# Recurrence levels 2 to 16 as products of 32 stationary and 16 moving columns

## Chip, core and metric

The kernel runs on one core of a Trainium2 chip. The metric is the device time of one execution in microseconds (us); lower is better. Three runs of the kernel before are given by their median, lowest and highest time. A profile is one further execution under the hardware profiler, with a time of its own.

## What is computed

The program is one block of a hybrid encoder: 512 tokens, model width 2048. A root-mean-square norm, one input projection of 5120 columns, a pooling mixer on the first 1024 of them, a gated linear recurrence (HGRN2) with 8 heads of 128 on the rest, an output projection, a residual, and a dense layer of 8192 with squared ReLU and a second residual. The change lies in the recurrence alone, whose part inside a chunk is a decayed score matrix:

```python
b = jnp.cumsum(g_c, axis=2)
o_inter = jnp.einsum('bhtd,bhde->bhte', q_c * jnp.exp(b), state)
diff = b[:, :, :, None, :] - b[:, :, None, :, :]
decay = jnp.exp(jnp.where(causal, diff, -jnp.inf))
scores = jnp.einsum('bhtd,bhsd,bhtsd->bhts', q_c, k_c, decay)
o_intra = jnp.einsum('bhts,bhse->bhte', scores, v_c)
```

The decay between a query t and a key s differs in each of the 128 channels d, so that the scores are not one plain product of q and k.

## The kernel before

**Order of the whole.** TensorE's work is, in order: ten groups of input projections (`pj`, line 251), four groups of output projections (`om`, line 251 too), and the dense layer's products (`mi`, `ps`, `al`, `ga`; lines 1059 to 1280). All of it is laid out by hand in program order; each engine runs its own instructions in that order and waits on semaphores.

**What runs between the projections.** A `Clock` holds generators ("tasks"). After each block of a projection group, which is twelve products of 128 x 128 stationary and 512 moving columns, `clock.tick()` advances every task by one step. The recurrence of four heads (a chunk `c` of the class `Hgrn`, two of them) is such a task: its `scores` generator begins once `evac_q` has its first block, and issues one step per tick. So each of its steps stands between two blocks of `pj` products on TensorE, and its VectorE and ScalarE work stands among the splitting of the projection weights into a high and a low part (`wh` on ScalarE, line 210; `wl` on VectorE, line 211).

**The score matrix by levels.** The 512 tokens are four windows of 128 (`NT` = 4). `ST` holds, per head and window, the 128 x 128 scores with keys on partitions and queries along the free axis. `LEVELS` is 1, 2, 4, 8, 16, 32, 64. At level m a window is cut into blocks of 2m tokens, and the second m tokens of a block (queries) meet the first m (keys). `decay` then multiplies queries and keys by the gates of a half block, so that after level m both carry the decay up to their block's border and level 2m can use them as they are. The diagonal and level 1 are made by column products and sums (`col_products`, `col_sums`), not by `level`.

**One burst of `level(m, hp)`** does a pair of heads, `hp`. For m up to 16 it issues 8 products (2 heads x 4 windows): all 128 keys of the window are stationary, and the 64 tokens that are queries at this level are the moving columns. Most of the 128 x 64 result is of no use; `merge` copies the wanted entries into `ST` on VectorE by `copy_predicated` with `masks[m]` (line 645). For m = 32 it issues 16 products of 32 stationary and 32 moving columns, written to the partitions 0 to 31 and 64 to 95 of the result; for m = 64, 8 products of 64 and 64. There ScalarE copies the wanted rows into `ST` (line 642). The result tile `lps` comes from the four rotating PSUM buffers of the pool `pss`. All these products are in plain float32, and the profile shows two weight loads and two matmul records for each of them.

**Around it.** A burst needs the queries and keys that the same pair's `decay` of the level before left, two ticks earlier; `decay` (lines 627, 629, 631 on VectorE) waits for the burst that read them. `ST` is read by `outputs` (products `po`, lines 679 and 681). GpSimd builds the masks and some edge values in the first microseconds, and has nothing else to do until the pooling mixer's second chunk and the first loads for the output stage.

Of the kernel before, what the change touches and what calls it, by code (L numbers as in the profile page):

```python
# [8 lines left out]
F32 = mybir.dt.float32  # L9
F32R = mybir.dt.float32r  # L10
U32 = mybir.dt.uint32
AF = mybir.ActivationFunctionType
ALU = mybir.AluOpType
# [3 lines left out]
P = 128  # L17
T = 512
NT = T // P
# [9 lines left out]
def hybrid_block(  # L29
# [20 lines left out]
    nc = tc.nc  # L50
# [17 lines left out]
    hgp = hg.__enter__()  # L68
    late = {}

    def junk_tile(shape, name):
        if "tp2" in late:
            return late["tp2"].tile(shape, F32, tag="junk", bufs=1, name=name)
        return hgp.tile(shape, F32, tag="junk", bufs=2, name=name)
# [11 lines left out]
    masks = {}  # L86
    for m in LEVELS[:-2]:
        nb = 64 // m
        mk = hgp.tile([P, nb, m], F32, name=f"mask{m}")
        nc.gpsimd.memset(mk, 1.0)  # L90
        nc.gpsimd.affine_select(out=mk, in_=mk, compare_op=ALU.is_ge, fill=0.0,
                                base=0, pattern=[[-2 * m, nb], [0, m]], channel_multiplier=1)
        nc.gpsimd.affine_select(out=mk, in_=mk, compare_op=ALU.is_ge, fill=0.0,
                                base=m - 1, pattern=[[2 * m, nb], [0, m]], channel_multiplier=-1)
        masks[m] = mk
    edge = {}
    for w in (2, 4, 8, 16):
        e = hgp.tile([P, w], F32, name=f"edge{w}")
# [425 lines left out]
    class Hgrn:  # L524
# [39 lines left out]
        def scores(self):  # L564
            F, Q, K = self.F, self.Q, self.K
            self.ST = hgp.tile([P, 4, NT, P], F32, tag="ST", name=f"ST{self.c}")

            sc = hgp.tile([P, 2, 2, 512], F32R, tag="V", name=f"sc{self.c}")

            def col_products(i, a, b):  # L570
                pr = junk_tile([P, 512], "pr")
                nc.vector.tensor_tensor(out=pr.rearrange("p (h x) -> p h x", h=a.shape[1]), in0=a, in1=b, op=ALU.mult)
                nc.scalar.copy(out=sc[:, i, 0], in_=pr)
                nc.vector.tensor_tensor(out=sc[:, i, 1], in0=pr, in1=sc[:, i, 0].bitcast(F32), op=ALU.subtract)

            def col_sums(i):
                ps = pss.tile([P, 512], F32, tag="s", name="cps")
                nc.tensor.matmul(ps, ones_r, sc[:, i, 0], start=True, stop=False)
                nc.tensor.matmul(ps, ones_r, sc[:, i, 1], start=False, stop=True)
                return ps  # L580

            def diag(h):
                nc.vector.tensor_tensor(out=self.ST[:, h], in0=col_sums(h % 2).rearrange("p (w t) -> p w t", t=P),
                                        in1=ident.unsqueeze(1).to_broadcast([P, NT, P]), op=ALU.mult)

            def halves(x, hp, k):
                return x[:, 2 * hp:2 * hp + 2].rearrange("p h (b two) -> p h b two", two=2)[:, :, :, k]

            for h in range(4):
                col_products(h % 2, Q[:, h:h + 1], K[:, h:h + 1])  # L590
                nc.vector.tensor_tensor(out=Q[:, h], in0=Q[:, h], in1=F[:, h], op=ALU.mult)
                yield 2
                diag(h)
            for hp in range(2):
                col_products(hp, halves(Q, hp, 1), halves(K, hp, 0))
                self.decay(1, hp)
                yield 2
                self.merge(1, hp, col_sums(hp))
            for m in LEVELS[1:]:
                for hp in range(2):  # L600
                    self.level(m, hp)
                    yield 1

        def level(self, m, hp):
            nb = 64 // m
            hs = slice(2 * hp, 2 * hp + 2)
            Q, K = self.Q[:, hs], self.K[:, hs]
            ps = pss.tile([P, 2, NT, nb, m], F32, tag="s", name="lps")
            mb = m if m >= 32 else P
            for h in range(2):  # L610
                for w in range(NT):
                    for r in range(0, P, 2 * m if m >= 32 else P):

                        b0, b1 = (r // (2 * m), r // (2 * m) + 1) if m >= 32 else (0, nb)
                        rhs = Q[:, h, w * P:(w + 1) * P].rearrange("p (b two i) -> p b two i", two=2, i=m)
                        nc.tensor.matmul(ps[r:r + mb, h, w, b0:b1], K[:, h, w * P + r:w * P + r + mb],  # L616
                                         rhs[:, b0:b1, 1, :], start=True, stop=True)
            self.decay(m, hp)
            self.merge(m, hp, ps.rearrange("p h w b i -> p (h w b i)"))

        def decay(self, m, hp):

# [748 lines left out]
    for k in range(n_in, len(slots)):  # L1371
        g, i, q = slots[k]
# [58 lines left out]
```

## Time and profile before

| what | value |
|---|---|
| median of three runs | 1961.36 us (1960.89 to 1961.70) |
| profiled execution, its own time | 1961.64 us |
| span of its instructions | 1959.9 us |
| TensorE matmul busy | 1941.4 us, 10040 records |
| VectorE busy | 1281.7 us |
| ScalarE busy | 841.9 us |
| GpSimd busy | 146.2 us |
| bursts of `lps` on TensorE | 172.2 to 429.3 us, 448 matmul records |

A matmul record is one pass of TensorE over the moving columns; its duration covers the whole way through the array, so that records of a dense stream overlap, and the distance from start to start is what one of them costs. Weight loads are listed as an engine of their own (PEld), since they run beside matmuls. A row of the timeline merges equal instructions that follow each other: its second column is the time from the first one's start to the last one's end.

### The profile page before, as it was taken

The page shows a single profiled execution, that of the slowest core. Times are in us where ns is not written, and L with a number is a line of the kernel's source. Part 1 is how long each engine was busy: PE and PEld are TensorE (multiplying, and loading weights), DVE is VectorE, ACT ScalarE, POOL GpSimd, SP SyncE. Part 2 cuts the span into 40 slices and gives each one's busy share as a digit, 9 for nine tenths or more (in the row PEclk, how much of TensorE's full clock was granted, in tenths as well). Part 3 has the DMA queues.
Part 4 walks back from the last instruction along what each step waited for, and adds up shares of the span by engine and source line. Part 5 has one row for each costly group of instructions (what it writes and reads, how often), then busy time and mean ns, then how long its engine had stood idle before and what let it go on. Part 6 is the DMA issues. An engine that isn't in the chain of part 4 may idle for free.

```text
span 1959.9 us, 24431 instructions
## 1 busy us (share of the span) xinstructions
PE 1941.4 (99%) x10040; PEld 1656.5 (85%) x10040; DVE 1281.7 (65%) x1414; ACT 841.9 (43%) x1009; POOL 146.2 (7%) x228
## 2 busy tenths in 40 slices
PE   9999999999999999999999999999999999999996
PEld 7888888888888899988888888888888888888885
DVE  5647543753632388566665766677777878878877
ACT  6221232223232277444444444445544444444454
POOL 1000000000000001101111011011010010010010
PEclk9999999999999999999999999999999999999999
DMA  8231213211252468988889789898897897898896
GB/s 312 86 106 67 83 68 108 86 65 65 100 212 86 148 200 180 248 233 203 216 219 213 226 215 207 240 235 238 211 245 225 199 235 230 206 229 223 217 228 134
DMA packets 56208, 355.00 MB, mean 181 GB/s; under 512 B 6048, under 2 KB 7072, under 8 KB 18336
## 3 DMA queue, kind: packets, MB, share of 16 engines
q0 software_dynamic: 25056, 162.54, 39.7%
q1 hardware_dynamic: 30752, 190.37, 26.5%
q8 instruction: 79, 1.29, 0.3%
q10 hardware_dynamic: 288, 0.52, 0.1%
q14 instruction: 33, 0.27, 0.0%
HBM read 328.24 MB, written 25.17 MB: 180 GB/s over the span
## 4 chain that ended last, share of the span: by engine, by line
PE 96%; DVE 1%; ACT 1%; issue 0%; DMA 0%; SPq 0%; DVEq 0%; ACTq 0%
PE pj L251 22%; PE ps L1059 18%; PE al L1280 17%; PE ga L1280 13%; PE ps L1062 9%; PE om L251 9%; PE mi L1074 4%; PE lps L616 2%; ACT mh L883 0%; DVE ml L884 0%; PE po L679 0%; PE fps L939 0%; DMA wr<-in_w_in 0%; PE po L681 0%; PE kvps L661 0%
## 5 line engine op out<-in xcount | busy, mean ns | idle before, releaser
L1059 PE MATMUL ps<-a,mh 128*128 128x512 f32 x1536 | 370.6, 391 | 0.0
L1059 PEld LDWEIGHTS ps<-a,mh 128*128 128x128 f32 x1536 | 281.0, 188 | 53.6 <-issue 0.3
L1280 PE MATMUL al<-mh,o 128*128 128x512 f32 x1024 | 317.1, 389 | 0.0
L883 ACT CAST mh<-X 128x1024 fp32r<-128x1024 f32 x176 | 180.2, 1052 | 202.7 <-PE ps L1059 82.9
L883 ACT CAST mh<-YX 128x1024 fp32r<-128x1024 f32 x176 | 180.5, 1054 | 159.5 <-PE ga L1280 44.3
L884 DVE TENSOR_TENSOR ml<-X,mh 128x1024 fp32r<-128x1024 f32 x176 | 207.4, 1220 | 55.3 <-ACT mh L883 55.1
L1280 PE MATMUL ga<-mh,o 128*128 128x512 f32 x768 | 237.8, 389 | 0.0
L251 PE MATMUL pj<-xT,wh 128*128 128x512 f32 x760 | 236.4, 392 | 0.7 <-ACT wh L210 0.7
L884 DVE TENSOR_TENSOR ml<-YX,mh 128x1024 fp32r<-128x1024 f32 x176 | 207.4, 1220 | 33.7 <-ACT mh L883 33.7
L1280 PEld LDWEIGHTS al<-mh,o 128*128 128x128 f32 x1024 | 192.3, 188 | 40.0 <-ACT mh L883 0.4
L211 DVE TENSOR_TENSOR wl<-wr,wh 128x1024 fp32r<-128x1024 f32 (+1 forms) x118 | 136.4, 1168 | 133.5 <-ACT wh L210 133.2
L1062 PEld LDWEIGHTS ps<-a,ml 128*128 128x128 f32 x1536 | 199.6, 191 | 9.0
L1062 PE MATMUL ps<-a,ml 128*128 128x256 f32 x1536 | 202.4, 283 | 0.0
L1280 PE MATMUL al<-ml,o 128*128 128x512 f32 x512 | 199.6, 390 | 1.1 <-DVE ml L884 1.0
L210 ACT CAST wh<-wr 128x1024 fp32r<-128x1024 f32 (+1 forms) x118 | 115.8, 1002 | 157.5 <-PE pj L251 73.1
L1280 PEld LDWEIGHTS ga<-mh,o 128*128 128x128 f32 x768 | 144.2, 188 | 29.8
L251 PE MATMUL pj<-wh,xT 128*128 128x512 f32 x512 | 168.9, 397 | 0.0
L251 PEld LDWEIGHTS pj<-xT,wh 128*128 128x128 f32 x760 | 141.5, 188 | 30.3 <-ACT wh L210 1.1
L1280 PE MATMUL ga<-ml,o 128*128 128x512 f32 x384 | 149.5, 389 | 0.0
L883 ACT CAST mh<-YZ 128x1024 fp32r<-128x1024 f32 x96 | 98.5, 1054 | 118.1 <-PE ps L1059 50.8
L251 PE MATMUL pj<-xT,wl 128*128 128x512 f32 x380 | 148.3, 390 | 0.0
L1108 DVE TENSOR_TENSOR t<-t,ps 128x512 f32<-128x512 f32 x120 | 82.5, 687 | 88.6 <-ACT t L1111 67.4
(221 smaller groups left out, 2536.2 us busy)
## 6 DMA issues: line engine op xcount, KB each, us to landing
wr<-in_w_in SPq DMA_DIRECT2D x38, 1024.0 KB, 4.8
X<-in_w_mlp_in POOLq DMA_DIRECT2D x33, 1024.0 KB, 9.2
X<-in_w_mlp_out POOLq DMA_DIRECT2D x33, 1024.0 KB, 9.7
YX<-in_w_mlp_in POOLq DMA_DIRECT2D x23, 1024.0 KB, 9.9
YX<-in_w_mlp_out POOLq DMA_DIRECT2D x23, 1024.0 KB, 9.8
YX<-in_w_mlp_in SPq DMA_DIRECT2D x21, 1024.0 KB, 5.4
YX<-in_w_mlp_out SPq DMA_DIRECT2D x21, 1024.0 KB, 4.9
wr<-in_w_out SPq DMA_DIRECT2D x16, 1024.0 KB, 4.8
```

What stands on the lines that cost most here:

```text
L210: nc.scalar.copy(out=hi[:, ks, :], in_=raw[:, ks, :])
L211: nc.vector.tensor_tensor(out=lo[:, ks, :], in0=raw[:, ks, :], in1=hi[:, ks, :].bitcast(F32), op=ALU.subtract)
L251: nc.tensor.matmul(bank, l, r, start=first and kt == 0 and oi == 0, stop=last and kt == 3 and oi == 2)
L616: nc.tensor.matmul(ps[r:r + mb, h, w, b0:b1], K[:, h, w * P + r:w * P + r + mb], rhs[:, b0:b1, 1, :], start=True, stop=True)
L883: nc.scalar.copy(out=hi[:, ks, :], in_=raw[:, ks, :])
L884: nc.vector.tensor_tensor(out=lo[:, ks, :], in0=raw[:, ks, :], in1=hi[:, ks, :].bitcast(F32), op=ALU.subtract)
L1059: nc.tensor.matmul(o, hi[:, kt, ms], r, start=first and kt == 0, stop=q == 1 and kt == 3 and not first, skip_group_check=True)
L1062: nc.tensor.matmul(o[:, 0], lo[:, kt, ms], r[:, 0], start=False, stop=q == 1 and kt == 3, skip_group_check=True)
L1074: nc.tensor.matmul(o, l[:, kt, ms], r[:, x], start=st and oi == 0 and m % 2 == 0, stop=sp and oi == 2, skip_group_check=True)
L1108: nc.vector.tensor_tensor(out=t, in0=t, in1=half(banks, s_), op=sign)
L1280: nc.tensor.matmul(bank[h] if type(bank) is list else bank[:, h, :], a[:, l, kt, ts], r[:, kt, :], start=i in (1, 2, 5) and kt == 0 and oi ...
```

## The change

For m up to 16 the two heads' products are cut into groups of 32 tokens. Since a block of 2m tokens is at most 32 long, each pairing of query and key at these levels stays inside one group of 32. A burst becomes 32 products (2 heads x 4 windows x 4 groups): 32 keys stationary, the group's 16 queries moving, the result written to the group's 32 partitions of a PSUM tile that is a quarter as wide. The masks are cut accordingly (`qmask`, 16 columns), and `copy_predicated` writes the wanted entries into a new tile `near`, which holds for each of the four groups on their own partitions only the 32 x 32 square at the diagonal; GpSimd clears it when `scores` begins. After level 16, `add_near` adds the four squares to `ST` on GpSimd. Levels 1, 32 and 64 stay as they were. The masks for m from 2 to 16 share one full-width buffer, since only their cuts are kept.

```diff
     for m in LEVELS[:-2]:
         nb = 64 // m
-        mk = hgp.tile([P, nb, m], F32, name=f"mask{m}")
+        mk = hgp.tile([P, nb, m], F32, tag="mask1" if m == 1 else "mask_all", name=f"mask{m}")
         nc.gpsimd.memset(mk, 1.0)
...
         masks[m] = mk
+        if m > 1:
+            masks[m] = hgp.tile([P, 16 // m, m], F32, name=f"qmask{m}")
+            for r in range(0, P, 32):
+                nc.gpsimd.tensor_copy(masks[m][r:r + 32], mk[r:r + 32, r // (2 * m):(r + 32) // (2 * m)])
...
             self.ST = hgp.tile([P, 4, NT, P], F32, tag="ST", name=f"ST{self.c}")
+            self.near = hgp.tile([P, 4, NT, 32], F32, tag="near", name=f"near{self.c}")
+            nc.gpsimd.memset(self.near, 0.0)
...
                     self.level(m, hp)
                     yield 1
+                if m == 16:
+                    self.add_near()
 
         def level(self, m, hp):
-            nb = 64 // m
+            nb = max(16 // m, 1) if m <= 16 else 64 // m
...
-            mb = m if m >= 32 else P
+            mb = max(m, 32)
             for h in range(2):
                 for w in range(NT):
-                    for r in range(0, P, 2 * m if m >= 32 else P):
-
-                        b0, b1 = (r // (2 * m), r // (2 * m) + 1) if m >= 32 else (0, nb)
-                        rhs = Q[:, h, w * P:(w + 1) * P].rearrange("p (b two i) -> p b two i", two=2, i=m)
-                        nc.tensor.matmul(ps[r:r + mb, h, w, b0:b1], K[:, h, w * P + r:w * P + r + mb],
-                                         rhs[:, b0:b1, 1, :], start=True, stop=True)
+                    rhs = Q[:, h, w * P:(w + 1) * P].rearrange("p (b two i) -> p b two i", two=2, i=m)
+                    for r in range(0, P, max(2 * m, 32)):
+                        b0 = r // (2 * m)
+                        b1 = b0 + max(16 // m, 1)
+                        o = ps[r:r + mb, h, w] if m <= 16 else ps[r:r + mb, h, w, b0:b1]
+                        nc.tensor.matmul(o, K[:, h, w * P + r:w * P + r + mb], rhs[:, b0:b1, 1, :],
+                                         start=True, stop=True)
             self.decay(m, hp)
-            self.merge(m, hp, ps.rearrange("p h w b i -> p (h w b i)"))
+            if m <= 16:
+                dst = self.near[:, hs].rearrange("p h w (b two i) -> p (h w) b two i", two=2, i=m)
+                nc.vector.copy_predicated(dst[:, :, :, 1, :],
+                                          masks[m].bitcast(U32).unsqueeze(1).to_broadcast([P, 8, nb, m]),
+                                          ps.rearrange("p h w b i -> p (h w) b i"))
+            else:
+                self.merge(m, hp, ps.rearrange("p h w b i -> p (h w b i)"))
+
+        def add_near(self):
+
+            for r in range(0, P, 32):
+                rs = slice(r, r + 32)
+                dst = self.ST[rs, :, :, rs].rearrange("p h w t -> p (h w) t")
+                nc.gpsimd.tensor_tensor(out=dst, in0=dst, in1=self.near[rs].rearrange("p h w t -> p (h w) t"),
+                                        op=ALU.add)
```

TensorE's rows around the first burst of level 8 in the first chunk, before. A row names the line, the operation, result and operands, the size of the result, and how many equal ones follow each other:

```order
L251 MATMUL pj_0_1071<-wl_1240,xT_157 128x512
L251 MATMUL pj_0_1071<-wh_1239,xT_157 128x512
L616 MATMUL lps<-Q_1006,K_831 128x64 x8
L251 MATMUL pj_1_1072<-wh_1239,xT_157 128x512
L251 MATMUL pj_1_1072<-wl_1240,xT_157 128x512
```

The same place after:

```order
L255 MATMUL pj_0_1093<-wl_1262,xT_177 128x512
L255 MATMUL pj_0_1093<-wh_1261,xT_177 128x512
L625 MATMUL lps<-Q_1026,K_851 32x16 x32
L255 MATMUL pj_1_1094<-wh_1261,xT_177 128x512
L255 MATMUL pj_1_1094<-wl_1262,xT_177 128x512
```

The burst keeps its place between the same two blocks of `pj`; its eight products have become 32. VectorE's rows behind the first burst of level 2, before (`Q`, `K` and `F` are the decay, `mask_98` is level 2's mask):

```order
L627 TENSOR_TENSOR Q_1006<-Q_1006,F_762 128x256x2
L629 TENSOR_TENSOR K_831<-K_831,F_762 128x256x2
L631 TENSOR_TENSOR F_762<-F_762 128x256
L645 COPY_PREDICATED ST_1012<-mask_98,lps 128x256x2
L211 TENSOR_TENSOR wl_1240<-wr_1190,wh_1239 128x1024
```

And after:

```order
L650 TENSOR_TENSOR Q_1026<-Q_1026,F_782 128x256x2
L652 TENSOR_TENSOR K_851<-K_851,F_782 128x256x2
L654 TENSOR_TENSOR F_782<-F_782 128x256
L630 COPY_PREDICATED near_1033<-qmask_102,lps 128x64x2
L215 TENSOR_TENSOR wl_1262<-wr_1212,wh_1261 128x1024
```

Nothing moved here; the masked copy handles 128 entries per partition where it handled 512, and its target is `near`. GpSimd's rows from the end of the first stage to the second chunk of the pooling mixer, before:

```order
L100 MEMSET edge_131 128x1 x16
L449 MEMSET pu_500 128x4x16
L449 MEMSET pu_3412 128x4x16
L762 DMA wpost_3723<-in_norm_mix_post 128x1024
L762 DMA wpost_3724<-in_norm_mix_post 128x1024
```

And after:

```order
L104 MEMSET edge_151 128x1 x16
L453 MEMSET pu_520 128x4x16
L572 MEMSET near_1033 128x512
L641 TENSOR_TENSOR ST_1032<-ST_1032,near_1033 32x16x32 x4
L572 MEMSET near_2556 128x512
L641 TENSOR_TENSOR ST_2555<-ST_2555,near_2556 32x16x32 x4
L453 MEMSET pu_3828 128x4x16
```

One clearing and four additions per chunk stand between the two clearings of `pu`. The `po` products of `outputs`, which read `ST`, now wait for GpSimd too; no other instruction of TensorE inside the recurrence does.

## Prediction

> **What bounds the kernel now.** I read the page first: the busy times and the chain of work that ended last, by engine and by line.
>
> ```profile
> PE 1941.4 (99%) x10040; PEld 1656.5 (85%) x10040; DVE 1281.7 (65%) x1414; ACT 841.9 (43%) x1009; POOL 146.2 (7%) x228
> PE 96%; DVE 1%; ACT 1%; issue 0%; DMA 0%; SPq 0%; DVEq 0%; ACTq 0%
> PE pj L251 22%; PE ps L1059 18%; PE al L1280 17%; PE ga L1280 13%; PE ps L1062 9%; PE om L251 9%; PE mi L1074 4%; PE lps L616 2%; ACT mh L883 0%; DVE ml L884 0%; PE po L679 0%; PE fps L939 0%; DMA wr<-in_w_in 0%; PE po L681 0%; PE kvps L661 0%
> ```
>
> TensorE is the chain from end to end, and `lps` at line 616, the products that the change touches, lies on it with 2%. So whatever these bursts gain or lose on TensorE should reach the end, if no other engine then comes late. How many bursts there are is read from the tile's own view:
>
> ```profile
> L616 PE MATMUL lps<-Q,K x448: 195/273/276, 172.4 to 429.3; 128*128 128x64 f32 x86, 128*32 128x32 f32 x42, 128*64 128x64 f32 x22
> L645 DVE COPY_PREDICATED ST<-mask,lps x16: 693/700/1314, 176.2 to 416.0; 128x512 f32<-128x512 uint32 x16
> ```
>
> There are 16 masked copies behind `lps`: 4 levels x 2 pairs of heads x 2 chunks, so 16 bursts change. Next the timeline of TensorE around one burst of level 16, which is one of the 16 (8 products, 16 records), and around one of level 32, which stays (16 products, 32 records). This level 32 row is the nearest that the trace has to what the change makes: its weights are already 32 columns wide and its results already stand on separate groups of 32 partitions.
>
> ```profile
> 203.71 0.39 PE L251 MATMUL pj<-wl,xT 128*128 128x512 f32 x1
> 203.94 0.40 PE L251 MATMUL pj<-wh,xT 128*128 128x512 f32 x1
> 204.17 1.89 PE L616 MATMUL lps<-Q,K 128*128 128x64 f32 x16
> 205.88 0.48 PE L251 MATMUL pj<-wh,xT 128*128 128x512 f32 x1
> 206.19 0.39 PE L251 MATMUL pj<-wl,xT 128*128 128x512 f32 x1
> 206.42 0.63 PE L251 MATMUL pj<-wh,xT 128*128 128x512 f32 x2
> 206.89 0.39 PE L251 MATMUL pj<-wl,xT 128*128 128x512 f32 x1
> ...
> 208.50 0.39 PE L251 MATMUL pj<-wh,xT 128*128 128x512 f32 x1
> 208.81 0.70 PE L616 MATMUL lps<-Q,K 128*32 128x32 f32 x32
> 209.44 0.50 PE L251 MATMUL pj<-wh,xT 128*128 128x512 f32 x1
> 209.78 0.39 PE L251 MATMUL pj<-wl,xT 128*128 128x512 f32 x1
> 210.01 0.62 PE L251 MATMUL pj<-wh,xT 128*128 128x512 f32 x2
> 210.47 0.40 PE L251 MATMUL pj<-wl,xT 128*128 128x512 f32 x1
> ...
> 215.96 1.15 PE L616 MATMUL lps<-Q,K 128*64 128x64 f32 x16
> ```
>
> **What a burst costs.** From the last `pj` before a burst to the fifth `pj` after it: level 16 takes 206.89 - 203.94 = 2.95 us, level 32 takes 210.47 - 208.50 = 1.97 us. Both hold five ordinary steps of `pj`, so only the difference counts. The level 32 burst carries costs that level 16 doesn't: its first record starts 0.31 us behind the last `pj` (0.23 at level 16), and the first `pj` behind it is followed after 0.34 us (0.31). They are inside the 1.97.
>
> The distance between records comes from a row's length, less the last record, over the steps. Level 16: (1.89 - 0.28) / 15 = 0.107 us for 128 stationary and 64 moving columns. Level 64: (1.15 - 0.22) / 15 = 0.062 us for 64 stationary and again 64 moving. With the moving side unchanged, half the weights take little more than half the time, so the weight load sets the pace in the wide form. A third step on that line would be about 0.031 for 32 columns. Level 32 shows (0.70 - 0.20) / 31 = 0.016 us, half of that. I read this as two column groups working side by side, each at about 0.032 us per record.
>
> **What the change makes of it.** The burst has 64 records where level 32 has 32, with weights of the same width and half the moving columns. The value I take is 0.016 us per record, as in the level 32 row: if the load of 32 weight columns sets the pace there, fewer moving columns change nothing; and since the two records of one product use the same column group one after the other, the second waits for its weights, and only its neighbour product can run beside it, so four groups do no better than two. The burst then costs 1.97 + 32 x 0.0163 = 2.49 us from `pj` to `pj`, against 2.95: **0.46 us less, x 16 = 7.4 us less**.
>
> The ends for this unknown: below, all four groups side by side, 0.032 / 4 = 0.008 us per record, 64 records as long as level 32's run: 1.97 us, 0.98 us less, x 16 = 15.7 us less. Above, no overlap at all, 0.0325 us: 1.97 - 0.50 + 63 x 0.0325 = 3.52 us, 0.57 us more, x 16 = 9.1 us more. Break-even is at (2.95 - 1.97 + 0.50) / 63 = 0.0235 us per record.
>
> The Trainium skill speaks against such a cut in "TensorEngine Tiling (Array Packing)", section Performance Considerations, under Instruction Overhead: a matmul has about 60 cycles of overhead, one moving column costs as much as 60, and no tiling factor should be taken from a side that is already small. By it, going from 64 to 16 moving columns earns nothing; the trace agrees in so far as I count nothing for the moving side, but the wide burst's time is in its 128 weight columns, which the rule doesn't look at. The page "TensorE: Matmul & The Clock Gate", section Back-to-back issue gap, gives a floor of about 25 ns between starts for up to 64 columns; 64 records at that would be some 0.1 us more per burst than now, about 2 us in all (an estimate), where the level 32 row stands at 16 ns, below that floor.
>
> **What the other engines do with it.** A tick, one block of `pj` and one burst, takes 4.54 us before and would take 4.08. The stretches between bursts, by engine (TensorE, weight loads, VectorE, ScalarE, GpSimd):
>
> ```profile
> 176.68:181.22 4.54, 4.54 (x30) 4.04 (x28) 4.20 (x6) 0.00 (x0) 0.00 (x0) 1.00 0.35 103
> 181.22:185.76 4.54, 4.54 (x30) 4.04 (x28) 3.11 (x5) 0.00 (x0) 0.00 (x0) 1.00 0.31 128
> 199.38:203.94 4.56, 4.56 (x30) 4.04 (x28) 3.01 (x6) 0.69 (x1) 0.00 (x0) 1.00 0.58 219
> sum 31.82, PE 31.82 PEld 28.30 DVE 20.73 ACT 5.55 POOL 0.00; mean PE 4.55 PEld 4.04 DVE 2.96 ACT 0.79 POOL 0.00
> ```
>
> VectorE has 2.96 us of work in a mean tick of seven. Only the first stretch is near: 4.20 us. That tick holds a level 2 masked copy:
>
> ```profile
> 180.71 1.30 DVE L645 COPY_PREDICATED ST<-mask,lps 128x512 f32<-128x512 uint32 x1
> 183.38 0.69 DVE L627 TENSOR_TENSOR Q<-Q,F 128x512 f32<-128x512 f32 x1 [1.37 <-PE lps L616]
> ...
> 184.71 0.42 DVE L631 TENSOR_TENSOR F<-F 128x128 f32<-128x128 f32 x1
> ```
>
> The copy now handles 128 entries instead of 512. Its cost lies between 0.3 us, a quarter of 1.30, and 1.30 as before; the nearest row of 128 strided entries is the decay's 0.42 us, which I take. The tick then has 3.3 us of VectorE work against 4.08. Were it still 4.20, VectorE would end 0.12 us late once, and the next tick with 3.11 takes that up. Its decay at 183.38 waited 1.37 us for the burst whose operands it changes; TensorE needs that decay only two ticks later, so a shorter or longer wait there reaches nobody. So the saved VectorE time is worth nothing, and costs nothing.
>
> **GpSimd** gets 16 small mask cuts at the start, two clearings and eight additions.
>
> ```profile
> L93 POOL TENSOR_SCALAR_AFFINE_SELECT mask<-mask 128x64 f32<-128x64 f32 x5 | 2.6, 529 | 0.3
> L83 POOL MEMSET ones<- 128x128 f32 x1 | 0.2, 199 | 0.0
> 8.80 0.15 POOL L449 MEMSET pu<- 128x64 f32 x1
> L460 DVE TENSOR_TENSOR pa<-pu x4: 1249/1250/1250, 55.4 to 523.8; 128x1054 f32<-128x1054 f32 x4
> 260.73 0.61 PE L679 MATMUL po<-V,ST 128*128 128x128 f32 x4
> ```
>
> The cuts cost at most 16 x 0.53 = 8.5 us, which moves the last start-up row from 8.80 to about 17 us; its reader on VectorE starts at 55.4. They cost nothing. Additions don't occur on GpSimd in this trace. One has 512 entries per partition: at the price of clearing 128 (0.2 us) four of them take 0.8 us, at that of the selection (0.53 us for 64 entries) 4 x 8 x 0.53 = 17 us; neither row is nearer, and I take some 4 us between them. They start behind level 16's last copy, about 208 us, and `po` starts at 260.7: even 17 us is hidden by the levels 32 and 64, the state products and the rest of the projection. The new wait of `po` for GpSimd is over long before it is asked. Queued behind it on TensorE would be the projections, so if the additions took over 50 us, all of the excess would count. ScalarE's copies at levels 32 and 64 write other squares of `ST`. GpSimd's own next work in the first chunk, and every DMA queue, stands where it stood.
>
> **Sum.** The profiled execution took 1961.64 us, 1.7 more than its span; 7.4 less is 1954.2. It stands 0.3 above the median of 1961.36, which becomes **1954.0**.
>
> **The rivals.**
> 1. *Four groups overlap fully.* For it: results go to four separate groups of partitions, and level 32 shows that two such groups overlap. Against: both records of a product want the same group. It gives 15.7 less: 1945.7. The Trainium skill leans this way: in "TensorE: Matmul & The Clock Gate", The mechanism (Part 3), matmuls of different tiles start about 4 ns apart; no row here shows four groups.
> 2. *Neighbours don't overlap.* Level 32 writes groups 64 partitions apart; the new order goes from one group to the next, 32 apart, and a record may have to wait for the one before. At 0.0325 us per record, TensorE is 9.1 us slower: 1970.5. It decides from 0.0235 us on. Against: nothing in the level 64 or level 32 rows shows such a tie.
> 3. *No change.* The pace lies near 0.0235 us, because starts come no closer in a long run of small products than in a short one, or TensorE's gain is lost in a new wait for VectorE. Half way between 0.0163 and 0.0325, at 0.0244 us, the burst costs 1.97 - 0.50 + 63 x 0.0244 = 3.01, so 0.9 us more in 16: 1962.3. Against: VectorE's slack above and the pace of the 32 records. The floor on starts in the Trainium skill ("TensorE: Matmul & The Clock Gate", Back-to-back issue gap) would end here too.
>
> **How the numbers follow.** The forecast gets 0.63: the 0.016 us row has the same weights, the same partitions and the same place between `pj` blocks. Rival 1 gets 0.18, rival 2 0.11, rival 3 0.08. A difference within 0.2% (3.9 us) can't be told from none. Faster is the forecast and rival 1, 0.81; same 0.08; slower 0.11. The forecast's own spread, 0.1 us per burst either way, is 1.6 us and some drift, 1951.5 to 1957; with rival 1 the range is 1945 to 1957, which holds 0.81.
>
> **What would show it.** Right: a level 16 burst of 64 records lasts about 1.2 us in the timeline and its `pj` to `pj` time is 2.49; masked copies near 0.4 us; no TensorE wait before `po`; VectorE's waits for `lps` shorter. Rival 1: 0.7 us. Rival 2: 2.2 us. Wrong altogether: TensorE idle before `lps` with VectorE as releaser, or bursts shorter while the end stays.

## The result, and the profile after

The changed kernel takes 1946.09 us (median of 4 runs, 1945.93 to 1946.43), the kernel before 1961.12 us beside it: ratio 0.9923, 95% interval 0.9906 to 0.9940. That is 15.0 us less. The forecast was 1954.0 us, 7.4 us less; the measured time lies inside the range of 1945 to 1957, at its lower edge, where rival 1 had put it, and outside the forecast's own spread of 1951.5 to 1957.

The page of the changed kernel, busy times and the chain by engine and line:

```profile
PE 1926.6 (99%) x10808; PEld 1636.9 (84%) x10808; DVE 1278.8 (66%) x1414; ACT 842.2 (43%) x1009; POOL 169.3 (9%) x254
PE 96%; DVE 2%; ACT 1%; issue 0%; DMA 0%; SPq 0%; DVEq 0%; ACTq 0%
PE pj L255 23%; PE ps L1082 18%; PE al L1303 17%; PE ga L1303 13%; PE ps L1085 9%; PE om L255 9%; PE mi L1097 4%; PE lps L625 1%; ACT mh L906 0%; DVE ml L907 0%; PE po L702 0%; PE fps L962 0%; PE po L704 0%; PE kvps L684 0%; DVE YT L1363 0%
```

TensorE is still the chain, with 768 matmul records more and 14.8 us less busy time. `lps` has gone from 2% to 1% of the chain. The timeline of TensorE around the second burst of level 16, the place that the prediction showed:

```profile
196.70 0.39 PE L255 MATMUL pj<-wh,xT 128*128 128x512 f32 x1
197.02 0.74 PE L625 MATMUL lps<-Q,K 128*32 128x16 f32 x64
197.69 0.50 PE L255 MATMUL pj<-wh,xT 128*128 128x512 f32 x1
198.02 0.40 PE L255 MATMUL pj<-wl,xT 128*128 128x512 f32 x1
198.26 0.63 PE L255 MATMUL pj<-wh,xT 128*128 128x512 f32 x2
198.72 0.39 PE L255 MATMUL pj<-wl,xT 128*128 128x512 f32 x1
```

From the last `pj` before the burst to the fifth behind it: 198.72 - 196.70 = 2.02 us, against 2.95 before and 2.49 forecast. The 64 records take (0.74 - 0.18) / 63 = 0.0089 us each, a little over half of the 0.0163 that I took. Sixteen times 0.93 us is 14.9 us: the bursts account for the whole change.

Three of the seven stretches between bursts, and the sum of all seven (TensorE, weight loads, VectorE, ScalarE, GpSimd):

```profile
171.40:175.05 3.65, 3.65 (x78) 2.81 (x76) 3.62 (x6) 0.00 (x0) 0.00 (x0) 1.00 0.00 0
175.05:178.68 3.63, 3.63 (x78) 2.81 (x76) 3.60 (x7) 0.00 (x0) 0.00 (x0) 1.00 0.31 72
178.68:182.31 3.63, 3.63 (x78) 2.81 (x76) 1.96 (x5) 0.00 (x0) 0.00 (x0) 1.00 0.56 219
...
sum 25.43, PE 25.43 PEld 19.69 DVE 18.54 ACT 3.94 POOL 0.00; mean PE 3.63 PEld 2.81 DVE 2.65 ACT 0.56 POOL 0.00
```

The view of the tile `near`, its copies on VectorE and additions on GpSimd (least, median and longest in ns):

```profile
L630 DVE COPY_PREDICATED near<-qmask,lps x16: 283/292/435, 175.0 to 400.4; 128x128 f32<-128x128 uint32 x16
L641 POOL TENSOR_TENSOR ST<-ST,near x8: 1619/1834/2267, 199.8 to 406.4; 32x512 f32<-32x512 f32 x8
```

A tick is now 3.63 us long, and VectorE has 2.65 us of work in a mean one; TensorE has no idle time in these seven stretches. In the first, which still holds a full-width copy of level 1, VectorE is busy for 3.62 of 3.65 us, and in the second, which holds none, for 3.60 of 3.63, so the cover is nearly used up in both.

### The profile page after: what moved, and what is told of

Its sections match the earlier page's. It is cut to its first block, busy times and chain, and to the rows that moved or that the text cites. A ratio compares the mean times of both kernels' runs of the same rounds, so it can differ in the third digit from the quotient of the medians.

```text
span 1944.3 us, 25995 instructions
## 1 busy us (share of the span) xinstructions
PE 1926.6 (99%) x10808; PEld 1636.9 (84%) x10808; DVE 1278.8 (66%) x1414; ACT 842.2 (43%) x1009; POOL 169.3 (9%) x254
## 4 chain that ended last, share of the span: by engine, by line
PE 96%; DVE 2%; ACT 1%; issue 0%; DMA 0%; SPq 0%; DVEq 0%; ACTq 0%
PE pj L255 23%; PE ps L1082 18%; PE al L1303 17%; PE ga L1303 13%; PE ps L1085 9%; PE om L255 9%; PE mi L1097 4%; PE lps L625 1%; ACT mh L906 0%; DVE ml L907 0%; PE po L702 0%; PE fps L962 0%; PE po L704 0%; PE kvps L684 0%; DVE YT L1363 0%
```

## The experiments

Two theories stood against each other. **Theory W**: inside one column group (one of the four sets of 32 partitions that a product can write) the width of the weights sets a record's pace, and all groups that are in the queue run side by side. **Theory M**: the moving columns set the pace, half as many take half the time, and never more than two groups run at once. Both give about 0.008 us per record for the change.

**Pairs of groups.** Same products, another order:

```diff
-            for h in range(2):
-                for w in range(NT):
+            for rows in (((0, 64), (32, 96)) if m <= 16 else (range(0, P, 2 * m),)):
+                for h in range(2):
+                    for w in range(NT):
...
-                    for r in range(0, P, max(2 * m, 32)):
+                        for r in rows:
```

> The products of the change in another order: first all that write partitions 0 to 31 and 64 to 95, in turn, then all of 32 to 63 and 96 to 127. Theory W (each column group takes 0.032 us per record, set by its 32 weight columns, and all groups that follow each other in the queue run side by side): two groups at a time, 0.016 us per record, 64 records in 1.0 us, burst from pj to pj 2.02 - 0.55 + 1.01 = 2.48 us as the prediction had it, total about 1953.5 us. Theory M (the moving side sets the pace, 16 columns take half of 32, never more than two groups at once): as the changed kernel, 0.0088 us per record, about 1946 us.

Measured: 1951.64 us, ratio 0.9950 (0.9936 to 0.9965). The burst's row on TensorE's timeline:

```profile
199.54 1.10 PE L626 MATMUL lps<-Q,K 128*32 128x16 f32 x64
```

(1.10 - 0.18) / 63 = 0.0146 us per record, where the same products in the changed kernel's order take 0.0089. With only two groups near each other in the queue a record takes nearly level 32's 0.0163 us, and 9.4 of the 15 us are still gained; the rest of the gain needs all four groups at once. Theory M is out.

**Neighbouring pairs**, the same with `((0, 32), (64, 96))`:

> As the run with groups 0 and 64 in turn, but the pairs are neighbours: first all products on partitions 0 to 31 and 32 to 63 in turn, then 64 to 95 and 96 to 127. If any two column groups run side by side: as that run, burst 2.38 us from pj to pj, 1951.6 us. If neighbours hinder each other (rival 2 of the prediction): up to 0.032 us per record, burst up to 3.2 us, up to 1964 us.

```profile
199.28 1.10 PE L626 MATMUL lps<-Q,K 128*32 128x16 f32 x64
```

The same row length, and 1951.68 us (ratio 0.9952, 0.9937 to 0.9966). For these two pairings it makes no difference which groups run side by side: neighbours don't hinder each other, as rival 2 had it.

**One group after another**, with `((0,), (32,), (64,), (96,))`:

> The products of the change, all of one column group after another (16 products on partitions 0 to 31, then 16 on 32 to 63, and so on). Theory W: no overlap but at the three borders, 0.032 us per record, 64 records in about 2.0 us, burst from pj to pj 3.5 us, 0.57 us more than before the change, about 1970 us: slower than before by some 9 us. Theory M: 16 moving columns at 0.016 us per record in one group, 1.0 us, about 1953.5 us.

Measured: 1964.46 us, ratio 1.0016 (1.0006 to 1.0025).

```profile
186.51 1.90 PE L626 MATMUL lps<-Q,K 128*32 128x16 f32 x64
```

The products of the change, in this order, are slower than the kernel before. Theory W had the direction but 1970 us. The row is 1.90 us long, 1.72 from first start to last, where 63 steps of 0.0325 (two of level 32's 0.0163) would be 2.05 us. Some nine or ten steps are missing. The starts of the single records, which the row merges, show where. Behind a first distance of 52 ns they follow each other by 31 to 32 ns, except at the three borders between groups: there seven distances alternate between 5 to 6 ns, three times, and 25 to 27 ns. So three pairs of records start nearly together at each border, and three steps are saved there: records of the next group appear to start while up to three of the group before still wait. With nine missing, a step is 1.72 / 54 = 0.0318 us. The same reading fits the pairs: 32 steps less three at their one border are 29 x 0.0318 = 0.92 us, which is that row's 1.10 - 0.18.

**More moving columns.** First all 32 tokens of a group instead of its 16 queries:

```diff
+                        q = rhs[:, b0:b1] if m <= 16 else rhs[:, b0:b1, 1, :]
-                        nc.tensor.matmul(o, K[:, h, w * P + r:w * P + r + mb], rhs[:, b0:b1, 1, :],
+                        nc.tensor.matmul(o, K[:, h, w * P + r:w * P + r + mb], q,
                                          start=True, stop=True)
```

> The changed kernel with 32 moving columns instead of 16: all tokens of the group, the unwanted half of the results is not copied. Theory W: the weights still set the pace, 64 records in about 0.55 us, total as the changed kernel, 1946 to 1947 us. Theory M: twice the time per record, burst 0.5 us longer, about 1954 us.

```profile
197.08 0.76 PE L628 MATMUL lps<-Q,K 128*32 128x32 f32 x64
```

1946.56 us, ratio 0.9925 (0.9910 to 0.9940). Twice the moving columns cost 0.02 us on a burst. Cutting them from 32 to 16 is worth next to nothing, as the prediction's central value had it. Then the kernel before with nothing but narrow weights, and 64 moving columns:

```diff
-            mb = m if m >= 32 else P
+            mb = max(m, 32)
...
-                    for r in range(0, P, 2 * m if m >= 32 else P):
+                    for r in range(0, P, 2 * m if m >= 32 else 32):
```

> The kernel before with its weights cut to 32 columns in four groups, and nothing else: 64 moving columns as before, the result tile, masks and copies into ST as before, no near and no additions. Theory W: a record then takes the longer of weights (0.032 us) and moving side (0.058 us as at level 64) in its group, four groups side by side, 0.0146 us per record, 64 records in 0.92 us, burst 2.39 us, about 1952.5 us. Theory M: two groups at once, 0.029 us, 1.85 us, burst 3.3 us, about 1967 us.

```profile
199.75 1.10 PE L616 MATMUL lps<-Q,K 128*32 128x64 f32 x64
```

1951.97 us, ratio 0.9952 (0.9937 to 0.9967), against 1952.5 expected. (1.10 - 0.22) / 63 = 0.014 us per record, four groups side by side, is 0.056 us in each group, near level 64's 0.062 with the same moving columns. So two lines of the diff, with the masks, copies and `ST` untouched, bring 9 of the 15 us; fewer moving columns bring nearly all of the other 6, by taking the moving side from 64 to 32, not from 32 to 16.

**The change without its products.** 8 wide products per burst as before, but copies into `near`, four per burst, and the additions on GpSimd:

```diff
+                for r in range(0, P, 32):
+                    rs, b0 = slice(r, r + 32), r // (2 * m)
+                    nc.vector.copy_predicated(dst[rs, :, :, 1, :], mk[rs], src[rs, :, b0:b0 + nb])
```

> The change without its products: 8 products of 128 stationary and 64 moving columns per burst as before, but the masked copies go into near (four per burst, one for each group of 32 partitions, 0.3 to 0.45 us each) and GpSimd adds near to ST. Theory that TensorE's burst alone makes the time: burst 2.94 us as before, 1961 us, at most a microsecond more at level 2, where VectorE's tick gets longer by some 0.4 us. Theory that the smaller copies or the additions have a part in the gain: below 1960 us.

```profile
199.35 1.89 PE L625 MATMUL lps<-Q,K 128*128 128x64 f32 x16
```

1961.15 us, ratio 1.0000 (0.9990 to 1.0009), and the burst as before. Beside the wide burst, the copies, the masks and the additions have no part in the time, within the 2 us of the interval either way.

**What sets the pace in the wide form.** The kernel before, each wide product cut into two of 32 moving columns:

```diff
+                        bm = (b0 + b1) // 2
+                        for c0, c1 in ((b0, bm), (bm, b1)) if m < 32 else ((b0, b1),):
-                        nc.tensor.matmul(ps[r:r + mb, h, w, b0:b1], K[:, h, w * P + r:w * P + r + mb],
-                                         rhs[:, b0:b1, 1, :], start=True, stop=True)
+                            nc.tensor.matmul(ps[r:r + mb, h, w, c0:c1], K[:, h, w * P + r:w * P + r + mb],
+                                             rhs[:, c0:c1, 1, :], start=True, stop=True)
```

> The kernel before, each of its 128-column products at levels 2 to 16 cut into two of 32 moving columns, with the same weights loaded for each: 32 records per burst. If the weight load sets the pace in the wide form: 0.11 us per record as before, burst 1.7 us longer, 16 x 1.7 = 27 us more, 1988 us. If the moving side does: 0.055 us per record, burst as before, 1961 us.

Two bursts of this run:

```profile
200.58 3.65 PE L618 MATMUL lps<-Q,K 128*128 128x32 f32 x32
...
206.92 4.17 PE L618 MATMUL lps<-Q,K 128*128 128x32 f32 x32
```

The first has (3.65 - 0.27) / 31 = 0.109 us per record, where twice the moving columns took 0.107: the 128 weight columns set the pace before. But the whole took 2002.3 us (ratio 1.0210, 1.0195 to 1.0225), 14 us more than the expected 1988, and the second burst is longer without having more to do. That comes from the clock (last section).

**What sets it in a narrow group.** The run with one group after another, with 16 weight columns per product (half of the keys' scores at levels 2 to 16 are left out, and the masked copy is made in four parts):

```diff
-            mb = max(m, 32)
+            mb = 16 if m <= 16 else m
```

> The run with one column group after another, with 16 instead of 32 weight columns per product: only the first 16 keys of each group of 32 are used, the scores of the other 16 at levels 2 to 16 are left out, and the masked copy is made in four parts of 16 partitions. If the weight columns set a group's pace of 0.032 us per record: about 0.018 us, the 64 records in about 1.0 us instead of 1.72, burst 2.5 us from pj to pj. If 0.032 us is a fixed least time of a record in its group: 1.72 us and 3.18 us as with 32 columns.

```profile
180.60 1.52 PE L626 MATMUL lps<-Q,K 128*16 128x16 f32 x64
```

1.52 - 0.18 = 1.34 us, between both expectations (1.0 and 1.72); the single run took 1958.93 us. Over the same 54 steps (63 less nine at the borders) that is 0.0248 us per record, where 32 columns take 1.72 / 54 = 0.0318; the single starts inside a group are 25 ns apart. So the weights do set the 0.032 us, but only 0.007 of it can be had: on the line through 128, 64 and 32 weight columns (0.109, 0.062 and 0.032 us) 16 would be near 0.018, and they stop at 0.025. The Trainium skill has such a floor in "TensorE: Matmul & The Clock Gate", section Back-to-back issue gap, about 25 ns between starts for up to 64 moving columns. This row agrees inside one group; four groups together start a record each 0.0089 us.

**Two bursts in one tick.** What a burst still pays beside its records is entering and leaving the narrow form, so both pairs of heads were put behind each other, and every second tick left without a burst:

```diff
                 for hp in range(2):
                     self.level(m, hp)
-                    yield 1
                 if m == 16:
                     self.add_near()
+                yield 2
```

> The changed kernel with both pairs of heads in one tick: the two bursts of a level stand behind each other, and the next tick has none. A burst pays for entering and leaving the narrow form (0.09 us more than an ordinary step before its first record, 0.11 us before the next pj, and 0.11 us behind that). Theory: 12 of the 24 bursts at levels 2 to 64 lose this, 0.3 to 0.36 us each, 4 us less than the changed kernel, 1942 us. Rival: the two decays of a level now stand together on VectorE (4 us) and the splitting of the weights waits behind them, TensorE waits for wl, and the gain is lost: 1946 us or more.

Measured: 1942.30 us, ratio 0.9906 (0.9891 to 0.9921). Both kernels were then run again on one chip:

> The changed kernel again, beside the version with two bursts per tick on the same chip: 1946 us.

> Both pairs of heads in one tick, again: 1942.3 us, 3.8 us less than the changed kernel on the same chip.

1946.17 us (0.9924, 0.9911 to 0.9938) and 1942.21 us (0.9903, 0.9890 to 0.9917) against 1961.09 us before: 4.0 us less, twelve times 0.33 us, as worked out. Its highest run, 1942.29 us, lies below the changed kernel's lowest, 1945.95. In the first series of four one run took 1944.13 us, below 1945.95 too. TensorE waits for no `wl` in this stage, so the rival's price wasn't paid. This version is faster than both kernels.

```profile
192.48 1.32 PE L625 MATMUL lps<-Q,K 128*32 128x16 f32 x128
```

128 records in (1.32 - 0.18) / 127 = 0.0090 us each: a queue of twice the length keeps the pace.

## Why the prediction was right, and where it was off

The direction and the bound were right, but the gain was twice the forecast. The time lies in the range only because the range took in rival 1, which had a chance of 0.18: the forecast's own spread misses 1946.09 us by 5.4 us.

- *TensorE bounds the stage, and what a burst gains reaches the end*: right. 16 x 0.93 = 14.9 of 15.0 us; the run without the new products took as long as the kernel before.
- *The wide burst's time is its 128 weight columns*: right, 0.107 us per record with 64 moving columns and 0.109 with 32.
- *Fewer moving columns than 32 change nothing*: right, 0.02 us per burst.
- *0.016 us per record, four groups no better than two*: **this term was mis-sized**, 0.0089 measured. The step that failed was "the second waits for its weights, and only its neighbour product can run beside it". It takes records to start strictly in program order, so that a product's waiting second record holds up all products behind it. The orders by pairs and by single groups show four groups, two, and one at 0.0089, 0.0146 and 0.0273 us per record, so each group has its own pace and the others pass. In the first half of the changed kernel's row the single starts come in rounds of four, 6 to 7 ns apart, and a round takes about 32 ns, the pace of one group alone. A strict order would allow one short distance at a border between groups, where the single-group row has three. The trace doesn't say which group a record belongs to; that the array itself picks records out of order is my reading of these starts. The level 32 row could not have told: with two groups, both readings give its 0.016.
- *Costs of entering and leaving*, taken over from level 32: right, 0.32 us to the first record, and 0.33 between the first two `pj` behind, as there.
- *VectorE*: the masked copy took 0.29 us, 0.43 at level 2, against 0.42 taken; the waits behind it cost nothing.
- *GpSimd*: four additions took 7.7 us against some 4 taken, inside the bounds of 0.8 and 17; `po` didn't wait, as it starts 45 us later. That they slow VectorE meanwhile was not foreseen (below), and was hidden too.
- *Rivals*: 1 came true to 0.7 us (15.7 forecast). 2's mechanism is excluded for the pairings tried; a slower kernel, though by 3.5 us and not 9.1, does appear when one group follows the other. 3 didn't happen.

## What to carry to other kernels

In these runs a burst of small products is paid by what its column groups do one by one: count records per group, times the larger price of its weight load and its moving side, and let consecutive products go to different groups, since the same products in a group-by-group order gave back more than the whole gain. Cutting weights from 128 to 32 columns over four groups was worth 9 us, cutting the moving side 6 more, nearly all of it from 64 to 32 columns, where the weights' price takes over. Where each burst pays for the change of form, put bursts together before making them shorter.

## What the runs showed of the hardware

**The clock.** In the run with cut wide products, the granted clock of TensorE (the column before the last two) falls where the bursts are, and recovers behind them. The third row holds the end of the second burst shown above, and the last is the kernel before:

```profile
172.00:230.00 58.00, 58.00 (x350) 52.12 (x349) 24.69 (x37) 5.55 (x7) 0.00 (x0) 0.85 0.11 37
230.00:400.00 170.00, 170.00 (x880) 141.22 (x879) 79.94 (x115) 47.60 (x61) 0.00 (x0) 1.00 0.25 85
209.90:216.70 6.80, 6.80 (x23) 5.64 (x22) 2.30 (x5) 0.29 (x1) 0.00 (x0) 0.50 0.46 154
...
172.00:216.00 44.00, 44.00 (x316) 38.01 (x314) 30.32 (x45) 8.04 (x12) 0.00 (x0) 1.00 0.19 66
```

TensorE counts as busy throughout, yet in bursts of 3.4 us it seems mostly to wait for weights: 0.109 us per record, where 32 moving columns ask for no more than the 0.032 of a narrow group. The clock falls in the stage that holds them, and not evenly: it is at half in pieces of 3.4 and 6.8 us, 17 us in the first chunk and 14 in the second, and at 1.00 between them, where a burst keeps its 3.65 us. Of the run's 41 us, 28 are the records' own pace (16 x 1.76), and the other 13 go with the clock; 31 us at half the clock can cost some 15. What lowers it was not tried further. The change's short bursts left it at 1.00.

**VectorE beside GpSimd.** The changed kernel's timeline of VectorE during the additions of the first chunk, and behind it that of GpSimd:

```profile
201.40 0.97 DVE L650 TENSOR_TENSOR Q<-Q,F 128x512 f32<-128x512 f32 x1 [0.71 <-PE lps L625]
202.29 1.79 DVE L652 TENSOR_TENSOR K<-K,F 128x512 f32<-128x512 f32 x1
204.11 1.14 DVE L654 TENSOR_TENSOR F<-F 128x16 f32<-128x16 f32 x1
205.17 1.21 DVE L215 TENSOR_TENSOR wl<-wr,wh 128x1024 fp32r<-128x1024 f32 x1
206.30 1.77 DVE L650 TENSOR_TENSOR Q<-Q,F 128x512 f32<-128x512 f32 x1
...
199.80 7.73 POOL L641 TENSOR_TENSOR ST<-ST,near 32x512 f32<-32x512 f32 x4 [182.53 <-DVE near L630]
```

The decay's products, 0.69, 0.68 and 0.19 us elsewhere, take 0.97, 1.79 and 1.14 us here, and the next pair's first 1.77: each seems to wait for an addition to end, and ends itself 0.05 to 0.55 us behind one of the four, which in the trace end at 201.82, 203.53, 205.20 and 207.53 us. Where VectorE is first it is the other way round: `wl` starts before the first and the fourth addition (the row at 205.17 is the second of them) and keeps its 1.2 us, while these two additions take 2.02 and 2.27 us, the other two 1.65 and 1.62. The Trainium skill says so in "SBUF — State Buffer", section Who interferes with whom: a VectorE instruction with two inputs in SBUF contends with a GpSimd instruction that reads SBUF, the ports that they share are an exclusive lock, and the order of issue decides who waits. The trace agrees: 3.4 us more on these four. It cost nothing here because TensorE asks for the decay two ticks later.
